# A length-masked softmax: one clip per batch over the upper columns, hand-written synchronisation, and loads whose width SyncE picks from the length

## The chip, the core and the metric

The kernel runs on one core of a Trainium2 chip. The core's engines each follow their own instruction stream: VectorE (DVE), ScalarE (ACT), GpSimd (POOL), SyncE (SP) and TensorE, which is not used here. Data moves between device memory and the on-chip memory (SBUF, 128 partitions) through 16 DMA engines. The metric is the device time of one execution in microseconds, as the median over runs.

## The reference

`x` has the shape 16 x 8 x 256 x 256 (batch, heads, query rows, key columns) in float32, which is 33.5 MB, and there is one length per batch. Each row's first `length` columns get a softmax, the rest are zero:

```python
batch, heads, seq_q, seq_k = 16, 8, 256, 256
x = np.random.randn(batch, heads, seq_q, seq_k)                  # float32
lengths = np.random.randint(seq_k // 2, seq_k, size=batch)       # 128 to 255
result = np.zeros_like(x)
for b in range(batch):
    length = lengths[b]
    masked = x[b, :, :, :length]
    exp_masked = np.exp(masked - np.max(masked, axis=-1, keepdims=True))
    result[b, :, :, :length] = exp_masked / np.sum(exp_masked, axis=-1, keepdims=True)
```

The draw is fixed. For the batches 0 to 15 the lengths are 188, 233, 229, 243, 195, 252, 165, 210, 222, 180, 209, 157, 159, 199, 214 and 248.

## The kernel before

One batch is one tile `x_tile` of 128 partitions x 16 rows x 256 columns, 2 MB. A partition holds 16 consecutive rows of `x`, so that its share is one contiguous run of 16 KB both in device memory and in SBUF. There are 12 slots for such tiles.

SyncE issues every large transfer on one queue, in the order of its program. First it issues the loads of batches 0 to 11 (L48). Then come the stores, one for each batch (L102), in the batch loop that starts at L63; behind the stores of batches 2 to 5 comes the load of batch 12 to 15 into a slot whose store has landed (L105). ScalarE's queue loads the lengths, broadcast to all partitions (L42).

VectorE makes a float row of column numbers plus 0.5 (L57), from numbers that GpSimd writes (L55), and a float copy of the lengths (L61). For each batch it then makes a row `cap` of 256 values (L67), (column + 0.5 - length) x -1e30: hugely positive below the length, hugely negative from it on. The minimum of `x` and `cap` (L80) leaves valid columns alone and pushes the others to a value whose exponential is 0. This clip is done in two halves of eight rows, 128 x 2048 elements each, over all 256 columns.

ScalarE takes the exponential of one row of 256 columns at a time and accumulates its sum (L87), 16 instructions for a batch. VectorE takes the reciprocals of eight sums (L93) and multiplies each row by its own (L95), eight instructions for a half. No maximum is subtracted in either kernel.

The Tile framework allocates the buffers, orders the instructions of an engine (it interleaves the halves and batches) and places the waits between engines.

Of the kernel before, what the change touches and what calls it, by code (L numbers as in the profile page):

```python
# [1 line left out]

# [4 lines left out]


F32 = mybir.dt.float32  # L10
ALU = mybir.AluOpType
EXP = mybir.ActivationFunctionType.Exp


@with_exitstack
def kernel(
    ctx: ExitStack,
    tc: tile.TileContext,
    x: bass.AP,
    lengths: bass.AP,  # L20
    out: bass.AP,
):
    nc = tc.nc
    P = nc.NUM_PARTITIONS

    batch, heads, seq_q, seq_k = x.shape
    rows = heads * seq_q
    assert rows % P == 0
    nt = rows // P

    x_f = x.rearrange("b h q k -> b (h q) k").rearrange("b (p t) k -> b p t k", p=P)
    out_f = out.rearrange("b h q k -> b (h q) k").rearrange("b (p t) k -> b p t k", p=P)

    slots = 12
    ahead = slots - 2

    singles = ctx.enter_context(tc.tile_pool(name="singles", bufs=1))
    work = ctx.enter_context(tc.tile_pool(name="work", bufs=slots))
    small = ctx.enter_context(tc.tile_pool(name="small", bufs=4))

    len_bcast = singles.tile([P, batch], mybir.dt.int64)
    nc.scalar.dma_start(out=len_bcast, in_=lengths.partition_broadcast(P))  # L42

    tiles = {}

    def load(b):
        tiles[b] = work.tile([P, nt, seq_k], F32, name="x_tile", tag="x_tile")
        nc.sync.dma_start(out=tiles[b], in_=x_f[b])  # L48

    for b in range(min(slots, batch)):  # L50
        load(b)


    iota_i32 = singles.tile([P, seq_k], mybir.dt.int32)
    nc.gpsimd.iota(iota_i32, pattern=[[1, seq_k]], base=0, channel_multiplier=0)  # L55
    iota_h = singles.tile([P, seq_k], F32)
    nc.vector.tensor_scalar(  # L57
        out=iota_h, in0=iota_i32, scalar1=0.5, scalar2=None, op0=ALU.add
    )
    len_f32 = singles.tile([P, batch], F32)  # L60
    nc.vector.tensor_copy(out=len_f32, in_=len_bcast.bitcast(mybir.dt.int32)[:, ::2])  # L61

    for b in range(batch):  # L63
        t = tiles.pop(b)

        cap = small.tile([P, seq_k], F32, name="cap", tag="cap")
        nc.vector.tensor_scalar(  # L67
            out=cap,
            in0=iota_h,
            scalar1=len_f32[:, b : b + 1],  # L70
            scalar2=-1.0e30,
            op0=ALU.subtract,
            op1=ALU.mult,
        )
        row_sum = small.tile([P, nt], F32, name="row_sum", tag="row_sum")
        inv_sum = small.tile([P, nt], F32, name="inv_sum", tag="inv_sum")
        half = nt // 2
        for h in range(2):
            s = slice(h * half, (h + 1) * half)
            nc.vector.tensor_tensor(  # L80
                out=t[:, s, :],
                in0=t[:, s, :],
                in1=cap[:, None, :].to_broadcast([P, half, seq_k]),
                op=ALU.min,
            )
            for j in range(h * half, (h + 1) * half):
                nc.scalar.activation(  # L87
                    out=t[:, j, :],
                    in_=t[:, j, :],
                    func=EXP,  # L90
                    accum_out=row_sum[:, j : j + 1],
                )
            nc.vector.reciprocal(out=inv_sum[:, s], in_=row_sum[:, s])  # L93
            for j in range(h * half, (h + 1) * half):
                nc.vector.tensor_scalar(  # L95
                    out=t[:, j, :],
                    in0=t[:, j, :],
                    scalar1=inv_sum[:, j : j + 1],
                    scalar2=None,
                    op0=ALU.mult,  # L100
                )
        nc.sync.dma_start(out=out_f[b], in_=t)  # L102
        n = b + ahead
        if b >= 2 and slots <= n < batch:
            load(n)  # L105


# [1 line left out]
_INS = ['x', 'lengths']  # L109
_OUTS = [((16, 8, 256, 256), 'float32')]  # L110


# [23 lines left out]
```

## Time and profile before

| | |
|---|---|
| Time, median of 3 runs | 166.28 us (166.01 to 166.45) |
| Profiled execution, its own time | 166.46 us |
| Span of its trace | 164.7 us |
| VectorE busy | 145.0 us, 88% of the span |
| ScalarE busy | 105.9 us, 64% |
| Large transfers (queue q1) | 67.11 MB, 96.5% of the span of 16 DMA engines |
| Mean rate of the DMA engines over the span | 408 GB/s |

The span runs from the first to the last record of the trace; the device time has 1.8 us around it. "Busy" counts only instructions that compute. The DMA share is the time that packets took, as a share of the time of 16 DMA engines; where it stands at 1.00, the engines had a packet at work all the time. A packet is one contiguous run that a DMA engine moves.

### The profile page before, as it was taken

What the parts mean: (1) busy time and instruction counts of PE and PEld (TensorE: products, weight loads), DVE (VectorE), ACT (ScalarE), POOL (GpSimd) and SP (SyncE); (2) the same over time, 40 slices, a digit from 0 to 9 for tenths busy, and PEclk for the clock granted to TensorE, in tenths of its full rate; (3) what the DMA queues carried; (4) which work ended last, traced back from release to release, by engine and by line L of the source; (5) the groups of instructions that cost most, each with busy time, mean ns of one, the idle gap of its engine ahead of it and who ended that gap; (6) DMA issues with size and microseconds to landing.
All of it is one profiled execution on the core that took longest, in us unless ns stands there. A gap on an engine that the chain in (4) does not pass through costs nothing.

```text
span 164.7 us, 981 instructions
## 1 busy us (share of the span) xinstructions
DVE 145.0 (88%) x338; ACT 105.9 (64%) x513; POOL 0.5 (0%) x5
## 2 busy tenths in 40 slices
DVE  0059999999999999999999999999999999999600
ACT  0038999177977476937887676937694887857200
POOL 1000000000000000000000000000000000000000
DMA  5999999999999999999999999999999999999693
GB/s 168 333 411 418 442 436 426 424 426 434 426 422 438 434 416 426 442 434 422 422 434 432 434 428 414 434 438 418 426 442 438 418 428 440 430 438 418 287 390 139
DMA packets 4759, 67.18 MB, mean 408 GB/s; under 512 B 656, under 2 KB 656, under 8 KB 656
## 3 DMA queue, kind: packets, MB, share of 16 engines
q1 hardware_dynamic: 4608, 67.11, 96.5%
q14 instruction: 7, 0.06, 0.1%
q10 hardware_dynamic: 144, 0.02, 0.1%
HBM read 33.57 MB, written 33.55 MB: 408 GB/s over the span
## 4 chain that ended last, share of the span: by engine, by line
DVE 86%; DMA 6%; ACT 2%; issue 1%; DVEq 0%; ACTq 0%
DVE x_tile L80 42%; DVE x_tile L95 39%; DMA len_bcast<-in_lengths_dram 6%; DVE inv_sum L93 2%; ACT x_tile L87 2%; DVE cap L67 2%; DVEq L131 0%; DVE iota_h L57 0%; DVE len_f L61 0%; ACTq L131 0%
## 5 line engine op out<-in xcount | busy, mean ns | idle before, releaser
L87 ACT ACTIVATE x_tile<-x_tile 128x256 f32<-128x256 f32 x256 | 102.5, 402 | 37.9 <-issue 23.3
L80 DVE TENSOR_TENSOR x_tile<-x_tile,cap 128x2048 f32<-128x2048 f32 x32 | 72.0, 2253 | 0.0
L95 DVE TENSOR_SCALAR x_tile<-x_tile,inv_sum 128x256 f32<-128x256 f32 x256 | 69.6, 339 | 0.1
L87 ACT ACTIVATION_READ_ACCUMULATOR x_tile<-x_tile 128x1 f32 x256 | 47.8, 187 | 0.0
L61 DVE CAST len_f<-len_bcast 128x16 f32<-128x16 int32 x1 | 0.2, 174 | 9.9 <-DMA len_bcast<-in_lengths_dram 9.9
L87 ACT ACT_TABLE_LOAD x1 | 1.3, 1283 | 9.8 <-DMA x_tile<-in_x_dram 9.8
L93 DVE RECIPROCAL inv_sum<-row_sum 128x8 f32<-128x8 f32 x32 | 5.9, 186 | 1.0 <-ACT x_tile L87 1.0
L67 DVE TENSOR_SCALAR cap<-iota_h,len_f 128x256 f32<-128x256 f32 x16 | 4.7, 309 | 0.0
L55 POOL IOTA iota_i<- 128x256 int32 x1 | 0.3, 342 | 0.4 <-PEq L131 0.4
L57 DVE TENSOR_SCALAR iota_h<-iota_i 128x256 f32<-128x256 int32 x1 | 0.3, 286 | 0.0
L120 POOL MEMSET const-bfloat16-1.0<- 128x1 bf16 x1 | 0.1, 102 | 0.0
L120 POOL MEMSET const-uint8-127<- 128x1 uint8 x1 | 0.1, 102 | 0.0
L120 POOL MEMSET const-float32-0.0<- 128x1 f32 x1 | 0.1, 99 | 0.2 <-issue 0.2
L120 POOL MEMSET const-float32-1.0<- 128x1 f32 x1 | 0.1, 99 | 0.0
## 6 DMA issues: line engine op xcount, KB each, us to landing
x_tile<-in_x_dram SPq DMA_DIRECT2D x16, 2048.0 KB, 26.1
out_dram<-x_tile SPq DMA_DIRECT2D x16, 2048.0 KB, 27.7
len_bcast<-in_lengths_dram ACTq DMA_DIRECT2D x1, 16.0 KB, 9.2
```

The lines of the kernel that those rows point to most:

```text
L55: nc.gpsimd.iota(iota_i32, pattern=[[1, seq_k]], base=0, channel_multiplier=0)
L57: nc.vector.tensor_scalar(out=iota_h, in0=iota_i32, scalar1=0.5, scalar2=None, op0=ALU.add)
L61: nc.vector.tensor_copy(out=len_f32, in_=len_bcast.bitcast(mybir.dt.int32)[:, ::2])
L67: nc.vector.tensor_scalar(out=cap, in0=iota_h, scalar1=len_f32[:, b : b + 1], scalar2=-1.0e30, op0=ALU.subtract, op1=ALU.mult,)
L80: nc.vector.tensor_tensor(out=t[:, s, :], in0=t[:, s, :], in1=cap[:, None, :].to_broadcast([P, half, seq_k]), op=ALU.min,)
L87: nc.scalar.activation(out=t[:, j, :], in_=t[:, j, :], func=EXP, accum_out=row_sum[:, j : j + 1],)
L93: nc.vector.reciprocal(out=inv_sum[:, s], in_=row_sum[:, s])
L95: nc.vector.tensor_scalar(out=t[:, j, :], in0=t[:, j, :], scalar1=inv_sum[:, j : j + 1], scalar2=None, op0=ALU.mult,)
L120: nc = _bacc.Bacc("TRN2", target_bir_lowering=False, num_devices=1)
```

## The change

- **Synchronisation by hand.** The kernel's body stands in one critical section, in which each engine's program order is as written and every wait is an explicit one on a semaphore. The buffers are allocated once. Sums and reciprocals have a place for each batch.
- **Lengths as register values.** SyncE and VectorE each load the 32 words of the lengths (16 values of 64 bits) from device memory into registers. On SyncE this stands behind the load of batch 0 and ahead of all other loads.
- **Loads by width.** For batches 1 to 15, SyncE compares the length with 144, 160, 176, 192 and 208, one compare after the other, and loads the first so many columns of every row for the first that covers it; all 256 columns, in the form as before, where none does. Batch 0 is loaded whole. With this draw, batches 4 and 13 get 208 columns, batch 6 gets 176, batch 9 gets 192, batches 11 and 12 get 160. A narrow load is 2048 separate runs (16 in each partition) of 640 to 832 bytes in place of 128 runs of 16 KB. Stores stay whole.
- **Filling.** GpSimd sets the columns from 144 on to zero in slots 1 to 11. Each of the first loads into these slots waits for its slot's fill.
- **Clip.** For a batch it covers the columns 128 to 255 of all 16 rows in one instruction, 128 partitions x 16 x 128 elements. A second clip, over columns 0 to 127, stands behind a branch that is only taken where the length is under 128; the lengths of this draw never are.
- **Order on VectorE.** The clip of batch b+1 stands ahead of the reciprocals and multiplications of batch b. The multiplications stay as they were, as do the exponentials on ScalarE.
- **Order on SyncE.** Loads 1 to 11, then the stores; behind the stores of batches 2 to 5 a wait until the store of batch b-2 has landed, and the load of batch b+10. At the end SyncE waits for every store.

The diff, cut to its core:

```diff
-    slots = 12
-    ahead = slots - 2
...
-    len_bcast = singles.tile([P, batch], mybir.dt.int64)
-    nc.scalar.dma_start(out=len_bcast, in_=lengths.partition_broadcast(P))
...
-    for b in range(min(slots, batch)):
-        load(b)
...
+    slots = min(12, batch)
+    behind = 2
+    widths = [144, 160, 176, 192, 208]
+    low = widths[0]
+    mid = seq_k // 2
...
+    with tc.tile_critical(no_gpsimd_drain=True):
...
+        nc.sync.dma_start(out=xt[0], in_=x_f[0]).then_inc(s_ld[0], 16)
+        nc.scalar.dma_start(out=len_i, in_=lengths.partition_broadcast(P)).then_inc(s_len, 16)
+
+        _, words = nc.values_load_multi_w_load_instructions(
+            lengths.bitcast(I32)[None, :],
+            engines=[SP, DVE],
...
+        )
+        lens = words[::2]
...
+            def go(w):
+                nc.sync.dma_start(out=t[:, :, :w], in_=x_f[b, :, :, :w]).then_inc(s_ld[b], 16)
+
+            def pick(ws):
+                if not ws:
+                    go(seq_k)
+                    return
+                with nc.sync.If(lens[b] <= ws[0]):
+                    go(ws[0])
+                with nc.sync.Else():
+                    pick(ws[1:])
+
+            pick(widths)
+
+        for b in range(1, slots):
+            nc.sync.wait_ge(s_fill, b)
+            load(b)
+        for b in range(batch):
+            nc.sync.wait_ge(s_out, b + 1)
+            nc.sync.dma_start(out=out_f[b], in_=xt[b % slots]).then_inc(s_st[b], 16)
+            n = b + slots - behind
+            if b >= behind and n >= slots and n < batch:
+                nc.sync.wait_ge(s_st[n - slots], 16)
+                load(n)
+        for b in range(batch):
+            nc.sync.wait_ge(s_st[b], 16)
...
+        for b in range(1, slots):
+            nc.gpsimd.memset(xt[b][:, :, low:], 0.0).then_inc(s_fill, 1)
...
-        for h in range(2):
-            s = slice(h * half, (h + 1) * half)
-            nc.vector.tensor_tensor(
-                out=t[:, s, :],
-                in0=t[:, s, :],
-                in1=cap[:, None, :].to_broadcast([P, half, seq_k]),
...
+        def clip(b, lo, hi):
+            t = xt[b % slots]
+            return nc.vector.tensor_tensor(
+                out=t[:, :, lo:hi],
+                in0=t[:, :, lo:hi],
+                in1=cap[:, b % 4, None, lo:hi].to_broadcast([P, nt, hi - lo]),
                 op=ALU.min,
             )
...
+        def mask(b):
+            if b + 1 < batch and b + 1 not in cap_at:
+                cap_at[b + 1] = make_cap(b + 1)
+            nc.vector.wait_ge(s_v, cap_at[b])
+            nc.vector.wait_ge(s_ld[b], 16)
+            with nc.vector.If(lens[b] < mid):
+                clip(b, 0, mid)
+            clip(b, mid, seq_k).then_inc(s_min, 1)
+
+        half = nt // 2
+        mask(0)
+        for b in range(batch):
+            if b + 1 < batch:
+                mask(b + 1)
+            t = xt[b % slots]
+            for h in range(2):
+                s = slice(h * half, (h + 1) * half)
+                nc.vector.wait_ge(s_exp, 2 * b + h + 1)
+                step(nc.vector.reciprocal(out=inv_sum[:, b, s], in_=row_sum[:, b, s]))
+                nc.vector.wait_ge(s_v, v)
...
```

## The prediction

> **What bounds the kernel now.** I read the page first: busy times, slices, queues, chain.
>
> ```profile
> DVE 145.0 (88%) x338; ACT 105.9 (64%) x513; POOL 0.5 (0%) x5
> ...
> DVE  0059999999999999999999999999999999999600
> DMA  5999999999999999999999999999999999999693
> ...
> q1 hardware_dynamic: 4608, 67.11, 96.5%
> ...
> DVE 86%; DMA 6%; ACT 2%; issue 1%; DVEq 0%; ACTq 0%
> ```
>
> Two resources are full from start to end. VectorE carries 86% of the chain that ended last, and the DMA engines are as full as it is. The chain names only one of them, so the stages have to be read by windows (length, busy times, clock, DMA share, GB/s):
>
> ```profile
> 0.00:10.00 10.00, 0.09 (x2) 0.21 (x1) 0.55 (x5) 1.00 0.80 275
> 20.00:60.00 40.00, 40.00 (x99) 28.95 (x143) 0.00 (x0) 1.00 1.01 428
> 60.00:100.00 40.00, 40.00 (x96) 29.51 (x144) 0.00 (x0) 1.00 1.01 430
> 100.00:150.00 50.00, 50.00 (x116) 36.00 (x176) 0.00 (x0) 1.00 1.01 430
> 152.00:154.00 2.00, 0.94 (x5) 1.56 (x8) 0.00 (x0) 1.00 0.96 410
> 154.00:156.00 2.00, 2.00 (x8) 0.00 (x0) 0.00 (x0) 1.00 0.52 221
> 156.00:158.00 2.00, 0.02 (x1) 0.00 (x0) 0.00 (x0) 1.00 0.69 295
> ```
>
> From 20 to 150 us the DMA share is 1.01 at 430 GB/s and VectorE is busy in every microsecond. Only from 154 us do the DMA engines go short, as the last store waits for VectorE. From SyncE's queue:
>
> ```profile
> 156.05 0.33 SPq L102 DMA_DIRECT2D out_dram<-x_tile  x1
> ```
>
> So I model the DMA side alone. One 2.097 MB transfer at 430 GB/s is 4.88 us; loads issued at 14.60, 19.49 and 24.39 us, each when a place came free, agree (4.89). In the first 10 us, 2.75 MB moved, 6.4 us of work: a loss of 3.6 us at the start. Then 32 x 4.89 = 156.5, and idle shares at 152 to 158 us of 0.1 + 1.0 + 0.6 = 1.7. The sum, 161.8, is where the bytes stop (the window from 162 us on has a share of 0.04). The span ends 2.9 us later. **VectorE's lateness costs only 1.7 us at present; removing any amount of VectorE work wins at most that, unless the DMA work shrinks too.**
>
> **What the Trainium skill says.** "DMA: Bandwidth & Descriptors", *Where 436 GB/s comes from*, gives 435 GB/s as the ceiling of a core's 16 DMA engines; the trace's 430 agrees. Its *Why small descriptors are slow* gives a fixed overhead of about 3 cycles for each packet, and "Advanced Engine Details and Errata", *Clock Domains*, 42 to 43 ns for a 1 KiB descriptor, so some 4 to 5 ns above 1024 bytes at the trace's rate. The trace allows a check: the lengths' transfer is the only one of small packets,
>
> ```profile
> q10 hardware_dynamic: 144, 0.02, 1.1%
> ```
>
> in the first 10 us: 1.1% of 160 us over 144 packets is 12.2 ns each. At 430/16 = 26.8 bytes per ns, 128 bytes are 4.8 ns, so 7.4 ns are overhead. On register loads, "Runtime: NRT & Kernel Launch", *Instruction fetch mechanics*, says about 200 ns a register even in bulk. No row of the trace shows one.
>
> **The change part by part.**
>
> *VectorE.* Two clips of 2.25 us become one of the same size (16 x 128 = 2048 elements): 16 x 2.25 = 36 us less. A batch is then cap 0.29 + clip 2.25 + 2 x (reciprocal 0.18 + multiplications about 2.15) = 7.2 us against 9.0 now (two batches take 18.0 us in the chain). The branch and the explicit waits come on top: about 0.1 us for the compare ("Advanced Engine Details and Errata", *Control Flow Timing*, 108 ns) and perhaps 0.1 us for each of five waits, 0.6 in all; unseen, I bound them by 0 and 1.2 us. ScalarE's 16 exponentials, 0.40 us apart, are 6.4 us a batch and lie beside it. Store 0 is ready near 22 us (below), store 15 near 22 + 15 x 7.8 = 139 us. The DMA queue needs it only near 153 us, so VectorE may take up to 8.7 us a batch unnoticed. The 1.7 us of idle go.
>
> *GpSimd.* 11 fills of 1792 elements. The nearest row is the iota, 0.34 us for 256 elements, so at most 2.4 us each; near one element per cycle it would be some 1.5 us. Fill b ends by 1.2 + 2.4b us, ahead of load b's turn from 9 us on, one per 4.9 us. Cost nothing; without that cover, the difference of a fill and a transfer, which is negative. "SBUF — State Buffer", *two separate sides*, has GpSimd share a port pair with some VectorE instructions; the fills end by 28 us, and the few microseconds that VectorE could lose there fall into its slack.
>
> *Start of SyncE.* Now 7 loads are issued by 4.6 us. After: load 0 at 0.74, then 32 register loads. At 0.2 us, 6.4 us. Behind them are queued all other loads, on VectorE the first clip; VectorE's own 6.4 us hide behind load 0, which lands near 9.8 us. SyncE is free at 1.1 + 6.4 = 7.5; the wait on the fill has passed; five failed compares are 0.54 us; from issue to first packets load 0 took 1.0 us. Load 1's packets start at 9.0 us. Load 0's bytes are through near 8.5. The loss at the start becomes 9.0 - 4.9 = 4.1 us, 0.5 more than now. Bounds: one round trip of about 1.3 us (the same skill page has that for a few words; no gap, -0.5) and the 600 ns for a load that the DMA page has as floor, if each word pays it (19.2 us, +12.8).
> Then load 1 lands near 15 us, its clip ends near 17.3, and batch 0's multiplications end near 22.
>
> *Loads.* 26 whole transfers (load 0, nine others, 16 stores): 26 x 4.89 = 127.1. The six narrow ones give each DMA engine 128 packets. At bytes / 26.8 + 7.4 ns: 832 bytes 38.4 ns, so 4.92 us (twice); 704 bytes 33.7, 4.31; 768 bytes 36.1, 4.62; 640 bytes 31.3, 4.00 (twice). Sum 26.8 against 29.3 whole: 2.5 us less for 3.5 MB. The 208-column loads save nothing. Bounds: no overhead gives 21.1 (-5.7). The upper one is the making of packets: an issue of 128 runs occupies SyncE 0.33 us, at most 2.6 ns a run, and if all of that scaled with runs, 2048 would take 5.3 us, 32.0 in all (+5.2 over my value). I take the packet price of the trace. SyncE is held during a narrow issue, but eight whole transfers could be outstanding before, so work is queued meanwhile.
>
> *Waits of SyncE for landed stores.* Four, like those that now cost SyncE 43.6 us while the DMA share stays at 1.01: nothing, since other stores and loads are queued. Without that cover, a gap of about 2 us each.
>
> *Sum.* 4.1 + 127.1 + 26.8 + 2.9 = 160.9 us span, against 164.7. With the 1.8 us around it, 162.7; the profiled run lies 0.2 above the median, so **162.5 us**, 2.3% less.
>
> **Rivals.**
>
> *A: the register loads are slow.* At 0.6 us a word, load 1 starts 12.8 us later with the DMA engines idle: 175.3 us, slower. It decides from 10.2 us of register loading (0.32 us a word), where my 3.8 us are spent. For it: they stand ahead of all loads but one. Against: the price of 0.2.
>
> *B: the narrow loads cost more than whole ones.* 5.3 us each is 167.7, slower by 1%. It decides from 0.63 us a load above my mean of 4.5. For it: 16 times the packets and no such load in the trace. Against: 7.4 ns already exceeds the skill's figure.
>
> *C: the narrow loads cost what whole ones do.* 165.0 us: only the idle tail is won.
>
> *D: VectorE stays the bound.* With waits and branches near 9 us a batch, store 15 comes near 157 as now: 164 to 167 us. Against: 1.8 us of additions are needed.
>
> That the change does not narrow anything is excluded by the lengths; the low clip is never run.
>
> **How the numbers follow.** Forecast 0.48, A 0.14, B 0.18, C 0.12, D 0.08. The forecast's own range is 160 to 165. The 80% range, 158.5 to 172, starts at cheap packets (7.4 ns down to 2) and takes in C, D, most of B and a little of A. No change means within 0.3%, about what a measurement can tell. Faster: 0.46 + 0.08 of C + 0.02 of D = 0.56; same 0.09; slower 0.35.
>
> **What would show it.** Right: VectorE near 109 us busy; DMA share about 1.0 from 10 us to the end; last store issued well ahead of the end; loads 2.5 us cheaper in packet time; load 1's packets by about 9 us. Wrong: idle DMA engines after load 0 (A); packets of 640 to 832 bytes above 40 ns, or issues of narrow loads above 4.5 us with the DMA share falling (B); VectorE busy or waiting on itself to the last store (D).

## The result, and the profile after

The changed kernel takes 168.19 us (median; 167.46 to 168.74) against 166.22 us before: a ratio of 1.0116, 95% interval 1.0071 to 1.016. It is slower by 1.2%, where 2.3% faster was forecast. Ratios and their intervals leave out runs more than 1.5% above the fastest run of the same kernel; only one experiment below has such runs. The profiled execution of the changed kernel took 168.74 us with a span of 167.0 us.

From the page of the changed kernel: busy times, slices of the span, and the queue of the large transfers.

```profile
DVE 118.7 (71%) x322; ACT 104.9 (63%) x513; POOL 17.8 (11%) x16
...
DVE  0049889999999999999999999999999400000000
...
DMA  2938999999999999999999999999999999999970
GB/s 78 390 82 330 426 436 382 395 412 297 425 420 366 382 394 406 432 430 428 342 447 362 427 436 381 428 430 438 428 428 424 432 428 436 436 432 428 428 314 39
...
q1 hardware_dynamic: 16128, 63.57, 95.3%
```

VectorE has stopped being a limit: it is done in slice 32 of 40. The bytes fell from 67.11 to 63.57 MB. Yet the span grew, and the DMA line shows one place where the time can be: the third slice, with a share of 3 and 82 GB/s. By windows (length, busy times of the engines with their instructions, clock, DMA share, GB/s) of the changed kernel:

```profile
0.00:10.00 10.00, 0.00 (x0) 1.28 (x1) 9.17 (x11) 1.00 0.55 211
10.00:20.00 10.00, 9.04 (x7) 2.16 (x11) 8.67 (x6) 1.00 0.80 297
...
8.00:10.00 2.00, 0.00 (x0) 0.00 (x0) 2.00 (x2) 1.00 0.33 139
10.00:12.00 2.00, 1.55 (x2) 0.00 (x0) 2.00 (x2) 1.00 0.00 0
12.00:14.00 2.00, 1.96 (x4) 0.00 (x0) 2.00 (x3) 1.00 1.02 246
14.00:16.00 2.00, 2.00 (x2) 0.00 (x0) 2.00 (x2) 1.00 0.99 401
```

By 20 us, 2.11 + 2.97 = 5.08 MB have moved; before, it was 2.75 MB by 10 us and 4.28 MB more by 20 us (428 GB/s). The line of the kernel before:

```profile
10.00:20.00 10.00, 9.96 (x12) 7.91 (x36) 0.00 (x0) 1.00 1.00 428
```

The deficit of 1.95 MB is 4.5 us at 430 GB/s. The engines stand still from about 8.7 us, on average, to the next packet at 12.2 us, and then restart slowly: 246 GB/s at a share of 1.02, so packets were at work but took long. What held the queue is the line of the register loads, L69 (engine, operation, count, then shortest/median/longest in ns, first and last start in us):

```profile
L69 DVEq TENSOR_LOAD <-in_lengths_dram_ptr x1: 905/905/905, 1.0 to 1.0; - x1
L69 SPq TENSOR_LOAD <-in_lengths_dram_ptr x1: 2393/2393/2393, 1.4 to 1.4; - x1
L69 DVEq TENSOR_LOAD <-in_lengths_dram x1: 8496/8496/8496, 1.9 to 1.9; - x1
L69 SPq TENSOR_LOAD <-in_lengths_dram x1: 6518/6518/6518, 3.8 to 3.8; - x1
```

On SyncE a load of the tensor's address takes 2.4 us and the load of the 32 words 6.5 us more. Five compares take another 0.8 us, and load 1 is issued at 11.17 us, against about 1.2 us before. From SyncE's queue, load 1 and, later, the last store:

```profile
11.17 1.49 SPq L81 DMA_DIRECT2D x<-in_x_dram  x2
...
131.21 0.33 SPq L99 DMA_DIRECT2D out_dram<-x  x1
```

The other end, in windows of 1 us of the changed kernel:

```profile
160.00:161.00 1.00, 0.00 (x0) 0.00 (x0) 0.00 (x0) 1.00 0.96 410
161.00:162.00 1.00, 0.00 (x0) 0.00 (x0) 0.00 (x0) 1.00 0.47 197
162.00:163.00 1.00, 0.00 (x0) 0.00 (x0) 0.00 (x0) 1.00 0.19 82
163.00:164.00 1.00, 0.00 (x0) 0.00 (x0) 0.00 (x0) 1.00 0.19 82
164.00:165.00 1.00, 0.00 (x0) 0.00 (x0) 0.00 (x0) 1.00 0.15 66
```

A share of 0.19 is three of sixteen DMA engines. The trace's landing records, one per DMA engine and transfer, say the same: of the last store, 13 shares have landed by 162.2 us, three land at 165.4 to 165.6. The last store was issued at 131.2 us, so nobody waited for VectorE. The span ends when the slowest DMA engine does. The kernel before had such stragglers too: its store 14 landed at 155.4 us in the median engine and at 159.0 in the slowest, and store 15 had been issued at 156.05, so the slowest engine still had work when the next store reached the queue. At its end two of sixteen engines were at work alone:

```profile
162.00:163.00 1.00, 0.00 (x0) 0.00 (x0) 0.00 (x0) 1.00 0.12 49
```

The DMA share is a mean of sixteen engines and adds up packets that overlap. A value near 1.00 therefore doesn't say that each engine had a packet at work all the time.

### The profile page after: what moved, and what is told of

Its sections match the earlier page's. It is cut to its first block, busy times and chain, and to the rows that moved or that the text cites. A ratio compares the mean times of both kernels' runs of the same rounds, so it can differ in the third digit from the quotient of the medians.

```text
span 167.0 us, 1053 instructions
## 1 busy us (share of the span) xinstructions
DVE 118.7 (71%) x322; ACT 104.9 (63%) x513; POOL 17.8 (11%) x16
## 3 DMA queue, kind: packets, MB, share of 16 engines
q1 hardware_dynamic: 16128, 63.57, 95.3%
## 4 chain that ended last, share of the span: by engine, by line
DVE 64%; DVEq 6%; ACT 4%; issue 4%; SPq 0%
DVE x L173 39%; DVE x L145 20%; DVEq L69 6%; ACT x L187 4%; DVE inv_sum L170 2%; DVE cap L130 2%; DVE len_f L123 1%; DVEq L157 0%; DVE iota_h L125 0%; DVEq L220 0%; SPq L53 0%
## 5 line engine op out<-in xcount | busy, mean ns | idle before, releaser
L187 ACT ACTIVATE x<-x 128x256 f32<-128x256 f32 x256 | 102.3, 402 | 22.2 <-DVE x L145 22.1
L173 DVE TENSOR_SCALAR x<-x,inv_sum 128x256 f32<-128x256 f32 x256 | 70.2, 349 | 1.1
L187 ACT ACTIVATION_READ_ACCUMULATOR x<-x 128x1 f32 x256 | 48.1, 188 | 0.0
L145 DVE TENSOR_TENSOR x<-x,cap 128x2048 f32<-128x2048 f32 x16 | 36.6, 2284 | 0.5 <-DMA x<-in_x_dram 0.5
L112 POOL MEMSET x<- 128x1792 f32 x11 | 17.4, 1630 | 0.0
L123 DVE CAST len_f<-len_i 128x16 f32<-128x16 int32 x1 | 1.7, 1677 | 10.5 <-issue 10.5
L130 DVE TENSOR_SCALAR cap<-iota_h,len_f 128x256 f32<-128x256 f32 x16 | 8.9, 563 | 0.0
L125 DVE TENSOR_SCALAR iota_h<-iota_i 128x256 f32<-128x256 int32 x1 | 1.7, 1726 | 0.0
```

The lines of the kernel that those rows point to most:

```text
L112: nc.gpsimd.memset(xt[b][:, :, low:], 0.0).then_inc(s_fill, 1)
L123: step(nc.vector.tensor_copy(out=len_f, in_=len32[:, ::2]))
L125: step(nc.vector.tensor_scalar(out=iota_h, in0=iota_i, scalar1=0.5, scalar2=None, op0=ALU.add))
L130: nc.vector.tensor_scalar(out=cap[:, b % 4, :], in0=iota_h, scalar1=len_f[:, b : b + 1], scalar2=-1.0e30, op0=ALU.subtract, op1=ALU.mult,)
L145: return nc.vector.tensor_tensor(out=t[:, :, lo:hi], in0=t[:, :, lo:hi], in1=cap[:, b % 4, None, lo:hi].to_broadcast([P, nt, hi - lo]), op ...
L173: ins = nc.vector.tensor_scalar(out=t[:, j, :], in0=t[:, j, :], scalar1=inv_sum[:, b, j : j + 1], scalar2=None, op0=ALU.mult,)
```

## The experiments

Each kernel was timed beside the kernel before, in 4 to 22 runs; ratios are to it. The diffs are cut to their core. The traces are of one execution each, which is not always near the median of its runs.

**Which part costs: narrow loads, register loads, or the rest.** Four kernels. The first keeps everything but loads whole:

```diff
-                nc.sync.dma_start(out=t[:, :, :w], in_=x_f[b, :, :, :w]).then_inc(s_ld[b], 16)
+                nc.sync.dma_start(out=t, in_=x_f[b]).then_inc(s_ld[b], 16)
...
-            pick(widths)
+            pick(widths[:1])
```

> The changed kernel with every load whole; register loads, one compare per load, fills and waits stay. Theory 1 (narrow loads save the average DMA engine 1.6 us, but three of the sixteen engines fall 3.5 us behind in them, and the last store waits for these): the lag goes, so about 166.5 us, and all engines end within 1 us of each other. Theory 2 (narrow loads are a gain, the lag has another cause in the new order): 169.5 to 170 us with the lag still there.

Measured: 170.75 us, ratio 1.0285 (1.0266 to 1.0305). Theory 1 falls: whole loads are slower, so the narrow ones are a gain of 1.7% (1.0285 - 1.0116), 2.8 us. It may be more, since this kernel makes one compare for a load in place of up to five, and issues load 1 at 10.47 us, 0.7 us earlier. The spread of the DMA engines is still there; the last store lands at 163.9 us in the median engine and at 167.7 in the slowest.

The second has the widths written into its program (`known` lists those that the changed kernel picks at run time):

```diff
-            engines=[SP, DVE],
+            engines=[DVE],
...
-            pick(widths)
+            go(known[b])
```

> The changed kernel with the widths of the loads known when the program is written: SyncE reads no lengths and compares nothing (so this kernel leaves the choice by length out on SyncE); VectorE still loads its registers. Theory 1 (the register loads hold SyncE from 1.4 to 10.4 us and leave the DMA engines idle from 8.7 to 12.0 us): load 1 follows load 0 at once, about 165.0 us. Theory 2 (some other limit holds the loads, such as fills or landing): 167.5 to 168.2 us.

Measured: 163.08 us, ratio 0.9831 (0.9812 to 0.9851). The gap is gone; from its windows:

```profile
8.00:10.00 2.00, 0.00 (x0) 0.00 (x0) 2.00 (x2) 1.00 0.99 401
10.00:12.00 2.00, 0.00 (x0) 0.00 (x0) 2.00 (x2) 1.00 1.01 434
12.00:14.00 2.00, 0.82 (x3) 0.00 (x0) 2.00 (x3) 1.00 1.07 459
```

The register loads on SyncE, with the compares, cost 1.0116 - 0.9831 = 2.85%, 4.7 us, more than the 3.2 us of theory 1. This one edit separates a loss from a gain. The first 20 us of this kernel:

```profile
0.00:10.00 10.00, 0.00 (x0) 1.28 (x1) 9.17 (x11) 1.00 0.59 234
10.00:20.00 10.00, 6.83 (x7) 0.62 (x3) 8.68 (x6) 1.00 1.02 437
```

These are 6.71 MB against 5.08 in the changed kernel, 3.8 us at 430 GB/s. The rest of the 4.7 us shows only at the end of the two traces, where the slowest DMA engine lags behind the median one by 1.5 us here and by 3.6 us in the changed kernel. Why it does was not found.

The third loads whole and at once (`known` is 256 for every batch), with no fills and no registers on SyncE:

```diff
-            engines=[SP, DVE],
+            engines=[DVE],
...
-            pick(widths)
+            go(known[b])
...
-            nc.sync.wait_ge(s_fill, b)
...
-        for b in range(1, slots):
-            nc.gpsimd.memset(xt[b][:, :, low:], 0.0).then_inc(s_fill, 1)
```

> All loads whole, issued at once as in the kernel before, no fills, no register loads on SyncE; the single clip, VectorE's register load and branch, and the waits by hand stay. Theory 1 (the DMA side alone sets the time; the clip wins the idle 1.7 us before the last store and nothing more): 164.5 us. Theory 2 (synchronisation by hand or the new order costs by itself): 166 us or more.

Measured: 166.87 us, ratio 1.0049 (1.0033 to 1.0065). Theory 2 is right: with half of the clip work gone and the loads issued at once as before, it is 0.8 us slower. Against the second kernel the narrow loads are worth 1.0049 - 0.9831 = 2.2%, 3.6 us (the fills, which only the second has, are in this difference).

The fourth issues loads 0 to 3 ahead of the register loads:

```diff
-        nc.sync.dma_start(out=xt[0], in_=x_f[0]).then_inc(s_ld[0], 16)
+        first = 4
+        for b in range(first):
+            nc.sync.dma_start(out=xt[b], in_=x_f[b]).then_inc(s_ld[b], 16)
...
-        for b in range(1, slots):
-            nc.sync.wait_ge(s_fill, b)
+        for b in range(first, slots):
+            nc.sync.wait_ge(s_fill, b - first + 1)
```

(with the fills starting at slot 4 as well)

> The changed kernel with loads 0 to 3 whole and issued ahead of the register loads (loads 1 to 3 are whole in the changed kernel too with these lengths); all else stays. Theory 1: the register loads are hidden behind 19 us of transfers, 165.0 us as with known widths. Theory 2: 167.5 to 168.2 us, as the compares and narrow issues later on SyncE are what delays.

Measured: 163.98 us, ratio 0.9897 (0.9873 to 0.9922). It still picks widths at run time, and it is faster than the kernel before and than the changed one. From the line of its register loads:

```profile
L71 DVEq TENSOR_LOAD <-in_lengths_dram x1: 13593/13593/13593, 1.9 to 1.9; - x1
L71 SPq TENSOR_LOAD <-in_lengths_dram_ptr x1: 2548/2548/2548, 3.5 to 3.5; - x1
L71 SPq TENSOR_LOAD <-in_lengths_dram x1: 10182/10182/10182, 6.0 to 6.0; - x1
```

The same 32 words take 10.2 us here, with four transfers queued, and 13.6 us on VectorE; in the third kernel, with all of them queued, VectorE's took 16.6 us. The 19 us of transfers hide the loads: load 4 is issued at 17.01 us, and the DMA share is 1.02 from 10 to 20 us. By the ratios this kernel is still 1.1 us slower than the one with known widths; where that lies was not found.

**Was VectorE's late end worth anything?** The kernel before with one edit, the clip over the upper half of the columns:

```diff
-                out=t[:, s, :],
-                in0=t[:, s, :],
-                in1=cap[:, None, :].to_broadcast([P, half, seq_k]),
+                out=t[:, s, 128:],
+                in0=t[:, s, 128:],
+                in1=cap[:, None, 128:].to_broadcast([P, half, seq_k - 128]),
```

> The kernel before with one edit: each clip covers the columns 128 to 255 only (1024 elements in place of 2048; with lengths of 128 or more the rest needs none). VectorE loses about 16 x 2 x 1.1 = 35 us of work. Theory 1 (the slowest DMA engine sets the end: its share of store 14 landed at 159.0 us in the kernel before, after store 15 had been issued at 156.05, so it never idled): within 0.3% of before, 165.7 to 166.2 us. Theory 2 (the forecast's step: the idle 1.7 us ahead of the last store goes): 164.2 us.

Measured: 166.09 us, ratio 0.9998 (0.9988 to 1.0008). From its page and its windows:

```profile
DVE 112.7 (69%) x338; ACT 104.4 (63%) x513; POOL 0.5 (0%) x5
...
154.00:156.00 2.00, 0.00 (x0) 0.00 (x0) 0.00 (x0) 1.00 1.02 434
156.00:158.00 2.00, 0.00 (x0) 0.00 (x0) 0.00 (x0) 1.00 0.99 426
158.00:160.00 2.00, 0.00 (x0) 0.00 (x0) 0.00 (x0) 1.00 0.86 369
160.00:161.00 1.00, 0.00 (x0) 0.00 (x0) 0.00 (x0) 1.00 0.16 66
161.00:162.00 1.00, 0.00 (x0) 0.00 (x0) 0.00 (x0) 1.00 0.11 49
162.00:163.00 1.00, 0.00 (x0) 0.00 (x0) 0.00 (x0) 1.00 0.12 49
```

32 us of VectorE work are gone, the idle share at 154 to 158 us is filled, and nothing is won: the median engine lands the last store 2 us earlier (160.3 against 162.3 us), the slowest at 163.6 against 163.7. Theory 1 holds. The idle time before was the time of the fast DMA engines.

**The price of the registers.** The changed kernel with every second word loaded:

```diff
-            lengths.bitcast(I32)[None, :],
+            lengths.bitcast(I32)[None, ::2],
...
-        lens = words[::2]
+        lens = words
```

> The changed kernel with registers loaded from every second word alone, 16 in place of 32 on each engine. Theory 1 (a fixed price for each register, 6.5 us for 32): the load takes 3.3 us on SyncE, load 1 is issued near 8 us, as load 0 ends, and the time falls to 164 us. Theory 2 (a price for the instruction, whatever it loads): 168.2 us.

Measured: 170.8 us, ratio 1.027 (1.0251 to 1.0289). Both theories missed. From the line of the register loads:

```profile
L69 SPq TENSOR_LOAD <-in_lengths_dram_ptr x1: 2602/2602/2602, 1.4 to 1.4; - x1
L69 SPq TENSOR_LOAD <-in_lengths_dram x1: 9115/9115/9115, 4.0 to 4.0; - x1
```

Half the registers take 9.1 us instead of 6.5: 0.57 us for each strided word against 0.20 us for each contiguous one. As a test of the start it works all the same: load 1 is issued at 13.97 instead of 11.17 us, 2.8 us later, and the kernel is 2.6 us slower.

**The price of a narrow load.** In the kernel with known widths, every load from batch 1 on is made 208, then 160 columns wide (by the entries of `known`):

```diff
-            pick(widths)
+            go(known[b])
```

> Known widths, no register load on SyncE, and every load from batch 1 on 208 columns wide, also where the length is larger (so the columns from 208 on are left out there, zero or stale). Theory 1 (bytes / 26.8 + 7.4 ns a packet, 4.92 us a load): as slow as whole loads, 166.9 us. Theory 2 (packets of a narrow load overlap in a DMA engine, so that the overhead falls to 3 to 4 ns, 4.4 to 4.5 us a load): 160 to 161 us.

> The same with every load from batch 1 on 160 columns wide (columns from 160 on left out). Theory 1 (4.00 us a load): 166.9 - 15 x 0.89 = 153.5 us. Theory 2 (overhead of 3 to 4 ns, 3.5 us a load): 146 us, where VectorE's pace of 7.1 us a batch may begin to count.

Measured: 164.23 us, ratio 0.9883 (0.9865 to 0.99), and 147.95 us, ratio 0.8879 (0.8854 to 0.8903). Against 166.87 us with whole loads, a load of 208 columns saves 2.64 / 15 = 0.18 us and one of 160 columns 18.9 / 15 = 1.26 us. Both lie between the theories. The windows of 10 to 50 us, in which nearly only loads run, first 208 columns:

```profile
10.00:50.00 40.00, 38.04 (x87) 32.08 (x160) 8.68 (x6) 1.00 1.11 355
```

and 160 columns:

```profile
10.00:50.00 40.00, 37.75 (x87) 32.09 (x160) 8.67 (x6) 1.00 1.12 357
```

1.704 MB at 355 GB/s are 4.80 us a load, 37.5 ns a packet; 1.311 MB at 357 GB/s are 3.67 us, 28.7 ns. Beyond bytes / 26.8 that leaves 6.5 and 4.8 ns. Shares of 1.11 and 1.12 show that packets of one DMA engine overlap, which the 7.4 ns of a single small packet didn't count. For the same reason the length of one packet's record overstates its price: those of 832 bytes last 41 ns on average, those of 640 bytes 32 ns.

**Two attempts at a better version, and one at the frame.** Four loads first, 16 words, no width of 208:

```diff
-    widths = [144, 160, 176, 192, 208]
+    widths = [144, 160, 176, 192]
...
```

> Loads 0 to 3 whole and ahead of the register loads, registers from 16 words, and 208 columns no longer among the widths (batches 4 and 13 are loaded whole). Theory 1 (208 columns cost what a whole load does, register loads are hidden already): 164.0 us, as with four loads first. Theory 2 (a load of 208 columns saves half a microsecond): 165 us.

Measured: ratio 0.9949 (0.9927 to 0.9971), from seven runs with a median of 164.85 us; five more took 167.12 to 168.66 us and are not in it (the median of all twelve is 165.94). Theory 2 fits: by the ratios it is 0.9 us slower than four loads first. The two loads of 208 columns explain 0.4 us of that, and the rest is open. Its longer register load (11.5 us on SyncE) leaves no gap in its trace: the DMA share stays between 0.96 and 1.04 from 6 to 20 us.

Whole loads at once, no register load, branch or low clip:

```diff
-        _, words = nc.values_load_multi_w_load_instructions(
...
-            with nc.vector.If(lens[b] < mid):
-                clip(b, 0, mid)
...
```

> Whole loads at once and no register load anywhere; the branch and the clip of columns 0 to 127 are left out. Theory 1 (the frame written by hand costs 0.9 us at its start and end, VectorE's register load of 16.6 us is off the path): 166.9 us. Theory 2 (VectorE's late start costs it): 165.9 us or less.

Measured: 166.74 us, ratio 1.0044 (1.0028 to 1.006). Theory 1 holds: VectorE's register load is off the path. What is written by hand (waits, order, one clip in place of two) costs about 0.7 us, as a clip over the same columns in the Tile kernel ran at 0.9998. Of the first 10 us:

```profile
0.00:10.00 10.00, 0.98 (x4) 1.28 (x1) 0.55 (x5) 1.00 0.66 252
```

2.52 MB against 2.75 MB before is 0.5 us; load 0 is issued at 0.94 instead of 0.74 us. At the end, this kernel and the third end 1.3 us after their last landing, the kernel before 0.9 us. But these two traces are of the fastest of their runs (166.02 and 166.34 us, below the 166.46 of the trace of the kernel before) and so don't hold the loss that the medians show. Where it lies is open.

Finer widths on top of four loads first, and no register load or branch on VectorE:

```diff
-    widths = [144, 160, 176, 192, 208]
+    widths = list(range(144, 209, 8))
...
```

> Loads 0 to 3 first and whole, widths from 144 to 208 in steps of 8 (batches 4, 6, 9 and 13 load 200, 168, 184 and 200 columns, 8 fewer than in the changed kernel), no register load, branch or low clip on VectorE (the clip of columns 0 to 127 is left out; no length of the reference's range needs it). Theory 1: four loads lose 32 bytes a packet, 4 x 128 x 1.2 ns = 0.6 us, so 163.4 us against 164.0 with four loads first. Theory 2 (the few bytes are lost in the spread of the DMA engines): 164.0 us.

Measured: 164.46 us, ratio 0.9907 (0.989 to 0.9923), no better than four loads first. The last store lands at 158.4 us in the median engine and at 161.6 in the slowest, against 157.5 and 159.8 there. The trace of four loads first is of its fastest run, though (162.94 us), and this one of its slowest (164.74), so they don't tell what the few bytes are worth. The 0.6 us of theory 1 were not seen; theory 2's cause isn't shown.

## Why the prediction was wrong

In differences of ratios times 166.2 us, the change is 0.8 us (frame by hand, third kernel) - 3.6 us (narrow loads) + 4.7 us (register loads and compares on SyncE) = 1.9 us. That this is the measured 1.16% is no check, as the three steps lead from kernel to kernel. The sizes are supported by other pairs: with whole loads the register loads cost 1.0285 - 1.0049 = 2.4%, 3.9 us (first against third kernel, with one compare and with the fills), and with register loads in place the narrow loads gain 2.8 us. Against the forecast's steps:

- **"VectorE's lateness costs only 1.7 us … The 1.7 us of idle go": failed.** The kernel with the upper clip alone shows a gain of 0. The mean share of 16 DMA engines was read as if they were one. A transfer is done when its slowest engine is, and that one lagged by 3.6 us at store 14 and had no idle time. The 2.9 us from the last bytes to the end went into the sum unchanged. They held the lag at the last store, only 1.5 us, since the fast engines had waited; with the wait gone (upper clip alone) it is 3.3 us.
- **"Start of SyncE", +0.5 us: right mechanism, wrong size.** It measured 4.7 us. The price from the Trainium skill's "Runtime: NRT & Kernel Launch", *Instruction fetch mechanics*, 0.2 us a register, is what the 32 contiguous words took (6.5 us). Missing in the sum were the load of the address ahead of it (2.4 us), 0.3 us of the compares, and the slow restart: from the first packet of load 1, at 12.2 us in place of the forecast 9.0, to 16 us 1.29 MB moved, an estimated 0.8 us less work than at 430 GB/s. Rival A named this place and its sign, idle DMA engines after load 0, was seen. It put the point from which it decides at 10.2 us of register loading; the 8.9 us measured lie below that. The point was set too high, since it counted on the 1.7 us, on a frame that costs nothing and on a restart at full rate.
- **"Loads", -2.5 us: right, and up to 1.1 us too small.** It measured -3.6 us against whole loads, and -2.8 us with register loads in place. The packet price from lone packets overstated the overhead: it is 4.8 ns for 640 bytes and 6.5 ns for 832. The forecast's other estimate, 4 to 5 ns from the 42 to 43 ns for 1 KiB in the Trainium skill's "Advanced Engine Details and Errata", *Clock Domains*, was closer. The upper bound on the making of packets did not come into play: SyncE's issues did last up to 12.9 us, but with the DMA engines at work. Rivals B and C fall, although one sign of B was there: packets of 704 bytes last 43 ns, but they overlap.
- **The frame by hand, left out of the sum without a reason: failed.** It measured 0.8 us (third kernel) and 0.7 us (without any register load). Which part of it costs this is open.
- **VectorE: right.** A batch takes 7.1 us (the clips at 34.11 and 41.25 us are one batch apart), below the 7.8 forecast with waits and branch, and the last store is issued at 131.2 us, forecast near 139. Rival D falls. The busy time is 118.7 us instead of 109; about 5 us of that go with instructions beside GpSimd's fills, as the third kernel, without fills, has 113.8 us.
- **GpSimd's fills and SyncE's four waits: right, hidden.** A fill took 1.63 us, and the DMA share lies between 0.98 and 1.07 from 20 to 160 us.

With the steps as measured, 162.5 + 1.7 + 4.2 - 1.1 + 0.8 = 168.1 us; again this must come out and adds no evidence. Why some DMA engines fall behind stays open. The lag is as large in kernels with whole loads (3.6 us before, 3.9 in the first experiment) as in the changed kernel (3.6), so the narrow loads are not its cause. In these three it grows in steps from about 0.5 us at load 0; with known widths it is 2.0 us from load 0 on and ends at 1.5.

## What to carry to other kernels

Where all transfers are spread over 16 DMA engines, the end is set by the slowest of them: look at how far apart the landings of one transfer are before counting an idle share near the end as something to win. A value read into an engine's registers held everything behind it in that engine's program, and here its wait grew with the traffic; issue enough transfers ahead of it to cover it. The gap in the DMA queue cost its length (about 3.5 us) and a slow restart.

## What the runs showed of the hardware

- A register load from device memory took 6.5 us for 32 contiguous words on SyncE with one transfer queued, 10.2 us with four; on VectorE 8.5 us, and 16.6 us with all loads queued. 16 strided words took 9.1 us on SyncE. The load of the address ahead of it took 0.9 us on VectorE and, on SyncE, 2.4 us in the changed kernel and 1.6 to 2.7 us in the others.
- Runs of 640 and 832 bytes loaded at 357 and 355 GB/s, whole partitions of 16 KB at 430.
- After a gap of about 3.5 us transfers ran at 246 GB/s in the window from 12 to 14 us, with the first packet at 12.2 us, and at 401 GB/s in the next 2 us.
- Next to GpSimd's fills, the conversion of the lengths on VectorE (128 x 16) took 1677 ns; without fills it took 175 ns (third kernel).
- The DMA engines of one core ended 32 equal transfers up to 4 us apart (163.9 and 167.7 us in the first experiment).
